# Squares of x summed by VectorE once all of x is there, and rotary tables of three mixers made behind x

## The chip, the cores and the metric

The kernel runs on one core of one Trainium2 chip. The metric is the device time of one execution in microseconds. In the rows, PE is TensorE's matmuls, PEld its weight loads, DVE is VectorE, ACT is ScalarE, POOL is GpSimd, and SP is SyncE, which here only issues the weights' DMAs. A name with a q behind it (SPq, ACTq, POOLq) is the queue of that engine.

## The reference

A sequence of 256 rows of 1024 floats (batch 1) goes through two blocks of four layers each, all in float32. In the first, every layer is a gated feed-forward part, a mixer (kinds A, B, C, A) and a second feed-forward part; in the second, a mixer (NSA, stick-breaking attention, convolution, MoBA) and an MLP.

```python
def rms_norm(x, g):
    return x * rsqrt(mean(x * x, -1) + 1e-6) * g
for i in range(4):                       # first block
    x = x + 0.5 * rms_norm(swiglu_ffn(rms_norm(x, g[0]), ...), g[1])
    x = x + rms_norm(mixer(rms_norm(x, g[2]), ...), g[3])
    x = x + 0.5 * rms_norm(swiglu_ffn(rms_norm(x, g[4]), ...), g[5])
for i in range(4):                       # second block
    x = x + mixer_2(rms_norm(x, attn_norm[i]), ...)
    x = x + square(relu(rms_norm(x, mlp_norm[i]) @ w_up)) @ w_down
```

Each of the 20 steps needs the sum of squares of x over the 1024 features of each row, and the three sub-parts of the first block also that of their own result. Mixer B turns queries and keys by tables of cosine and sine that come from an input of positions; NSA and MoBA normalise every head by its own root mean square, with a gain, and turn it by tables that the kernel has as constants.

## The kernel before

x stays in SBUF, transposed: `self.x` is [128, 8, 256], eight parts of 128 features by 256 rows. A float32 product is made of two halves of each side in three matmuls (`mm3`): `xThi` is x times the gain, rounded by ScalarE, and `xTlo` the rest, by VectorE; each weight tile comes by a DMA on SP's queue into `raw` (three buffers), ScalarE rounds it into `whi` and VectorE makes `wlo` (four buffers each). `wlo` of 128x512 is what VectorE mostly does.

A step ends in `handoff`. Where its result is normalised (a *gated* step, the twelve of the first block), `normed` gets the factor of each row, and then, part by part, VectorE multiplies the result by it (`yg<-yg,ps`) and adds it to x (`x<-x,yg`), ScalarE makes `xThi` and VectorE `xTlo`. The first four parts come one by one (128x256), the last four in two pairs (128x512). In the second block `add_y` does that in pairs, without a factor. The first matmuls of the next step (`arriving`) use the parts in the order in which they come, so TensorE can wait for each `xThi` and `xTlo`.

For the next step's row factor, `rest_x` squares each pair of parts on ScalarE (into `acc` for the first pair, into `sq` then) and `add_squares` adds it to `acc` on GpSimd: three additions of 128x512 per step. `rms` folds `acc` on GpSimd (128x256), then TensorE sums over the partitions (`col_sums`, `ps<-ones,acc`), VectorE makes `e` (mean plus a small number) and GpSimd `r = e ** -0.5`. In a feed-forward step TensorE soon turns `r` into a row over the partitions (`to_rows`, `ps<-identr,r`); in a mixer `r` scales what leaves PSUM, and in NSA and MoBA `hrx`, `rs_e`, `rs_r` and `hrs` are the factors of single heads, `rope_a` and `rope_b` the two products of a rotation, added on GpSimd and then transposed by TensorE.

In mixer B, `rope_positions` makes the tables on VectorE from `pos_i`; in NSA and MoBA `gained_rope` multiplies the constants by the gains (`qtc`, `qts` for queries; `ktc`, `kt0c` and so on for keys). Both stand in the code ahead of the first projections. Temporaries lie in `temp()`, which is the buffer `yg` (there is one).

The order on each engine is not written out. Tasks (`spawn`) are generators; `tick` after each `mm3` advances those whose time has come by a planner (`Clock`, a table of modelled costs per engine), `after` waits for other tasks, and a scheduler behind it orders each engine's queue by those modelled times. So an instruction that changes its engine also changes where others stand. Nearly every operation is recorded by one helper, so its line is L163 throughout.

Of the kernel before, what the change touches and what calls it, by code (L numbers as in the profile page):

```python
# [17 lines left out]
P = 128  # L18
D = 1024
S = 256  # L20
# [180 lines left out]
class Net:  # L201
# [337 lines left out]

    def new_stats(self):  # L540
        self.acc = self.nrm.tile([P, 2, S], F32, name="acc", bufs=1)
        self.e = self.small.tile([P, 2], F32, name="e", bufs=3)
        r = self.small.tile([P, 2], F32, name="r", bufs=3)
        self.r2, self.r = r, [r[:, t:t + 1] for t in range(2)]
# [8 lines left out]
    def rest_x(self, ks, g):  # L553

        nc = self.nc
        hi, lo = self.xTs
        for k in ks:
            ins = nc.vector.scalar_tensor_tensor(lo[:, k], self.x[:, k], self.gcol[:, k, g:g + 1], hi[:, k].bitcast(F32),
                                                 op0=ALU.mult, op1=ALU.subtract)
            if k % 2:  # L560
                self.add_squares(self.acc, self.x[:, k - 1:k + 1], k == 1)
        self.have[1] = ks[-1] + 1
        return ins

    def leave(self, b):

        x = self.x[:, 2 * b:2 * b + 2]
        for t in range(2):
# [5 lines left out]
            self.nc.sync.dma_start(self.a["out"][0, t * P:(t + 1) * P, b * S:(b + 1) * S], z)  # L574

    def arriving(self):

        for k in range(KB + LATE):
            for part, i in ((0, k), (1, k - LATE)):
                if 0 <= i < KB:  # L580
                    self.until(lambda: self.have[part] > i)
                    yield from [(i, 0, 1)] if part else [(i, 0, 0), (i, 1, 0)]

    def add_squares(self, acc, x, first, engine=None):
        nc = self.nc
        sq = acc if first else self.nrm.tile([P, 2, S], F32, name="sq", bufs=2)
        nc.scalar.activation(sq, x, AF.Square)
        if not first:
            (engine or nc.gpsimd).tensor_tensor(acc, acc, sq, op=ALU.add)

# [26 lines left out]
    def rms(self, deps):  # L617

        nc = self.nc
        yield from self.after(deps)  # L620
        nc.gpsimd.tensor_tensor(self.acc[:, 0], self.acc[:, 0], self.acc[:, 1], op=ALU.add)
        yield
        pc = self.bank()[:, :2]
        self.col_sums(pc, [self.acc[:, 0]], True, True)
        nc.vector.tensor_scalar(self.e, pc, 1.0 / D, EPS, op0=ALU.mult, op1=ALU.add)
        nc.gpsimd.tensor_tensor(self.r2, self.e, self.mhalf[:, :2], op=ALU.pow)
# [51 lines left out]
    def gain_y(self, y, ds, g, o):  # L678

        nc = self.nc  # L680
        b = ds[0] // 2
        acc = o["acc"]
        if len(ds) == 2:
            self.add_squares(acc, y[1][b], b == 0, nc.vector)
            if b == 2:
                nc.vector.tensor_tensor(acc[:, 0], acc[:, 0], acc[:, 1], op=ALU.add)
        else:
            sq = self.nrm.tile([P, 2, S], F32, name="sq", bufs=2)[:, 0]
            nc.scalar.activation(sq, y[0][ds[0]], AF.Square)
            if ds[0] == 6:  # L690
                o["add"] = nc.vector.tensor_tensor(acc[:, 0], acc[:, 0], sq, op=ALU.add)
            else:
                o["last"] = sq
        for d in {(4, 5): (), (6,): (4, 5, 6), (7,): ()}.get(ds, ds):
            ins = nc.vector.tensor_scalar(self.yg[:, d], y[0][d], self.gcol[:, d, g:g + 1], None, op0=ALU.mult)
            if d >= 4:
                self.behind(ins, o["add"])
        return
        yield

    def normed(self, y, o, g_out, g_next, weight, rest):
# [16 lines left out]
        rows = self.to_rows(r, WARM, last)  # L718
        self.new_stats()
        before = None  # L720
# [356 lines left out]
    def rope_positions(self, c):  # L1077
# [3 lines left out]
        nc.scalar.dma_start(pi, self.a["positions"].rearrange("o (t p) -> p (o t)", p=P))  # L1081
        pf = c.tile([P, 2], F32, name="pos_f")
        nc.vector.tensor_copy(pf, pi)
        tmp = self.temp()
        ang, kq, r, w = [tmp[:, i * 64:(i + 1) * 64].rearrange("p (t d) -> p t d", t=2) for i in range(4)]
# [192 lines left out]
    def mixer_b(self, mp, m1, j, kv, end):  # L1278
        nc = self.nc
        self.rope_positions(m1)  # L1280
        tabs = [m1.tile([P, 2, 64], F32, name=f"tab{t}") for t in range(2)]
# [45 lines left out]
        for jp in range(2):  # L1327
# [3 lines left out]
            for z, dst in enumerate((qT, kT)):  # L1331
                memory(jp * 3 + z)
                for t, ps in self.chunk(384):
                    if jp == 0 and z == 0:
                        for i, tab in enumerate((self.cos1, self.sin1)):
                            nc.vector.tensor_scalar(tabs[t][:, i], tab[:, t], self.r[t], None, op0=ALU.mult)
# [118 lines left out]

    def gained_rope(self, pool, gain, name):

        nc = self.nc
        c, s = [pool.tile([P, 2, P], F32, name=name + z) for z in "cs"]
        tab = lambda z: self.k[z].rearrange("p (t d) -> p t d", t=2)  # L1460
        half = lambda i: gain[:, i * 64:(i + 1) * 64].unsqueeze(1).to_broadcast([P, 2, 64])
        for i in range(2):
            nc.vector.tensor_tensor(c[:, :, i * 64:(i + 1) * 64], tab("cos2"), half(i), op=ALU.mult)
        nc.vector.scalar_tensor_tensor(s[:, :, :64], tab("sin2"), -1.0, half(1), op0=ALU.mult, op1=ALU.mult)
        nc.vector.tensor_tensor(s[:, :, 64:], tab("sin2"), half(0), op=ALU.mult)
        return c, s

# [20 lines left out]
    def nsa(self, mp, m1, stack, end):  # L1488
# [3 lines left out]
        cp = cctx.enter_context(self.tc.tile_pool(name="cmp", bufs=1))  # L1492
        tmp = self.temp()
        kg, qg = tmp[:, :3 * P], tmp[:, 3 * P:4 * P]
        nc.gpsimd.dma_start(qg, a["nsa_q_norm_2"][0].partition_broadcast(P))
        nc.gpsimd.dma_start(kg, a["nsa_k_norm_2"][0].rearrange("i d -> (i d)").partition_broadcast(P))
        qtab = self.gained_rope(m1, qg, "qt")
        ktab = [self.gained_rope(cp, kg[:, i * P:(i + 1) * P], f"kt{i}") for i in range(3)]
        kcT = cp.tile([P, 2, S], F32, name="kcT")
# [18 lines left out]

        def key(t, ps, tab, out):
            r = self.head_rms(ps, 2, t)  # L1520
            k = self.rope(mp, ps, 2, P, tab[0][:, t], tab[1][:, t])
# [228 lines left out]
    def moba(self, mp, m1, stack, end):  # L1750
        nc, a = self.nc, self.a
        sc = P ** -0.5
        gq, gk = [self.bcast_row(m1, a[f"moba_{n}_norm_2"][0], n + "g") for n in "qk"]
        qtab, ktab = self.gained_rope(m1, gq, "qt"), self.gained_rope(m1, gk, "kt")
        self.new_parts(m1, 8)

        def key(t, ps, out):
            r = self.head_rms(ps, 4, t)
            k = self.rope(mp, ps, 4, P, ktab[0][:, t], ktab[1][:, t])
# [56 lines left out]
    def prepare_conv(self, pool):  # L1816
# [6 lines left out]

        def weights():
            tmp = self.temp()[:C]
            nc.scalar.dma_start(tmp[:W], a["conv_dw_w_2"][0])
            for i, name in enumerate(("dw_b", "ln_g", "ln_b")):
                nc.scalar.dma_start(tmp[W + i:W + i + 1], a[f"conv_{name}_2"])
            yield from self.after([self.stats])
            self.clock.wait(self.clock.now() + 4 * DMA)  # L1830
# [222 lines left out]
```

## Time and profile before

| | |
|---|---|
| median of 3 runs | 3267.43 us (3265.96 to 3268.48) |
| profiled execution, its own time | 3249.1 us |
| its span, from first to last instruction | 3247.3 us |
| mean clock granted to TensorE | 0.992 |
| busy: TensorE, VectorE, ScalarE, GpSimd | 3176.4, 2109.8, 1663.0, 230.1 us |

The profiled execution is a single one, and its own time stands beside the span of the profile; durations are read from it, while times of kernels are compared by medians of runs. An engine with a small share can still hold up others at one place, so the share is read first and the order of time afterwards.

### The profile page before, as it was taken

What the parts mean: (1) busy time and instruction counts of PE and PEld (TensorE: products, weight loads), DVE (VectorE), ACT (ScalarE), POOL (GpSimd) and SP (SyncE); (2) the same over time, 40 slices, a digit from 0 to 9 for tenths busy, and PEclk for the clock granted to TensorE, in tenths of its full rate; (3) what the DMA queues carried; (4) which work ended last, traced back from release to release, by engine and by line L of the source; (5) the groups of instructions that cost most, each with busy time, mean ns of one, the idle gap of its engine ahead of it and who ended that gap; (6) DMA issues with size and microseconds to landing.
All of it is one profiled execution on the core that took longest, in us unless ns stands there. A gap on an engine that the chain in (4) does not pass through costs nothing. (4 is left out here: it accounts for less than half of the span.)

```text
span 3247.3 us, 60685 instructions
## 1 busy us (share of the span) xinstructions
PE 3176.4 (98%) x25234; PEld 3028.7 (93%) x25234; DVE 2109.8 (65%) x3877; ACT 1663.0 (51%) x3396; POOL 230.1 (7%) x205
## 2 busy tenths in 40 slices
PE   8999999999999999999999999999999999999999
PEld 8998999998999997899998998799989999997998
DVE  5657757566757556665757756775667576657754
ACT  6445545444545445544545544645565464545643
POOL 1001000001000000000001001200102010002100
PEclk9999999999999999999999999999999999999999
DMA  7654555544454643365554654536545551554463
GB/s 265 209 195 156 169 195 171 193 130 149 155 193 155 212 157 124 117 208 182 183 195 137 196 195 136 182 104 195 177 162 175 189 182 40 189 188 154 140 201 130
DMA packets 387971, 550.89 MB, mean 170 GB/s; under 512 B 12109, under 2 KB 310957, under 8 KB 387695
## 3 DMA queue, kind: packets, MB, share of 16 engines
q1 hardware_dynamic: 372648, 534.89, 50.4%
q10 hardware_dynamic: 14694, 10.92, 1.1%
q8 instruction: 198, 3.24, 0.4%
q0 software_dynamic: 352, 1.19, 0.2%
q14 instruction: 79, 0.64, 0.1%
HBM read 543.82 MB, written 3.15 MB: 168 GB/s over the span
## 5 line engine op out<-in xcount | busy, mean ns | idle before, releaser
L163 ACT CAST whi<-raw 128x512 fp32r<-128x512 f32 x1996 | 1119.1, 617 | 1041.5 <-issue 870.4
L163 DVE TENSOR_TENSOR wlo<-raw,whi 128x512 fp32r<-128x512 f32 x1996 | 1307.6, 700 | 509.7 <-ACT whi L163 508.7
L163 PE MATMUL ps<-xThi,whi 128*128 128x256 f32 x3904 | 1037.7, 278 | 3.3 <-ACT xThi L163 3.3
L163 PE MATMUL ps<-xTlo,whi 128*128 128x256 f32 x3904 | 1033.9, 277 | 4.5 <-DVE xTlo L163 4.5
L163 PE MATMUL ps<-xThi,wlo 128*128 128x256 f32 x3904 | 1032.8, 277 | 0.0
L163 PEld LDWEIGHTS ps<-xTlo,whi 128*128 128x128 f32 x3904 | 713.3, 188 | 6.4 <-DVE xTlo L163 5.9
L163 PEld LDWEIGHTS ps<-xThi,whi 128*128 128x128 f32 x3904 | 713.0, 188 | 6.7 <-ACT xThi L163 6.1
L163 PEld LDWEIGHTS ps<-xThi,wlo 128*128 128x128 f32 x3904 | 713.5, 188 | 0.0
L163 PE MATMUL ps<-hTlo,whi 128*128 128x256 f32 x2176 | 602.8, 277 | 0.0
L163 PE MATMUL ps<-hThi,wlo 128*128 128x256 f32 x2176 | 602.7, 277 | 0.0
L163 PE MATMUL ps<-hThi,whi 128*128 128x256 f32 x2176 | 602.7, 277 | 0.0
L163 PEld LDWEIGHTS ps<-hThi,wlo 128*128 128x128 f32 x2176 | 409.6, 188 | 0.0
L163 PEld LDWEIGHTS ps<-hThi,whi 128*128 128x128 f32 x2176 | 409.4, 188 | 0.0
L163 PEld LDWEIGHTS ps<-hTlo,whi 128*128 128x128 f32 x2176 | 409.4, 188 | 0.0
L163 PE MATMUL ps<-whi,xThi 128*128 128x512 f32 (+4 forms) x688 | 255.1, 386 | 4.6 <-ACT xThi L163 4.6
L163 PE MATMUL ps<-whi,xTlo 128*128 128x512 f32 (+4 forms) x688 | 245.4, 372 | 4.7 <-DVE xTlo L163 4.7
L163 PE MATMUL ps<-wlo,xThi 128*128 128x512 f32 (+4 forms) x688 | 245.0, 372 | 2.0 <-DVE wlo L163 1.9
L163 DVE TENSOR_TENSOR act<-ps,rows 128x512 f32<-128x512 f32 x88 | 60.7, 690 | 179.2 <-PE ps L163 179.2
L163 DVE TENSOR_TENSOR h<-ps,act 128x512 f32<-128x512 f32 x88 | 60.8, 690 | 149.3 <-PE ps L163 145.7
L163 PEld LDWEIGHTS ps<-whi,xTlo 128*128 128x128 f32 x688 | 130.5, 191 | 26.5 <-DVE xTlo L163 7.3
L163 PEld LDWEIGHTS ps<-whi,xThi 128*128 128x128 f32 x688 | 130.1, 192 | 26.0 <-ACT xThi L163 8.2
L163 POOL TENSOR_TENSOR acc<-acc,sq 128x512 f32<-128x512 f32 x60 | 95.1, 1586 | 828.2 <-issue 637.3
(332 smaller groups left out, 3495.5 us busy)
## 6 DMA issues: line engine op xcount, KB each, us to landing
raw<-in_ffn_w_gate_up_dram SPq DMA_DIRECT2D x176, 1024.0 KB, 5.1
raw<-in_ffn_w_down_dram SPq DMA_DIRECT2D x88, 1024.0 KB, 4.9
raw<-in_mlp_w_up_dram SPq DMA_DIRECT2D x64, 1024.0 KB, 5.5
raw<-in_mlp_w_down_dram SPq DMA_DIRECT2D x64, 1024.0 KB, 4.9
raw<-in_a_w_in_dram SPq DMA_DIRECT2D x12, 1024.0 KB, 5.2
raw<-in_sb_w_in_dram SPq DMA_DIRECT2D x12, 1024.0 KB, 5.1
raw<-in_moba_w_in_dram SPq DMA_DIRECT2D x12, 1024.0 KB, 5.1
raw<-in_b_w_in_dram SPq DMA_DIRECT2D x36, 256.0 KB, 3.7
```

Of the source, the lines that this page charges most:

```text
L163: return f(*args, **kw)
```

## The change

GpSimd no longer adds squares. ScalarE writes the squares of all four pairs into `yg`; when all of x is there, VectorE adds the eight parts in place in three additions (128x1024, 128x512, 128x256), and TensorE sums what is left. In the gated steps `yg` is the buffer out of which the same parts of x were just made. The tables of mixer B, NSA and MoBA become tasks of their own that begin when all of x has been split (`arrived`), in tiles `sq` instead of `yg`; NSA's gains come by ScalarE's DMA queue instead of GpSimd's, and MoBA's keys and NSA's keys wait for the tables (`tabled`). The convolution's small weights are fetched behind the statistics. The diff, cut to its core (the calls of the gates' own `add_squares`, which ran on VectorE already, only lose an argument):

```diff
-    def new_stats(self):
-        self.acc = self.nrm.tile([P, 2, S], F32, name="acc", bufs=1)
+    def new_stats(self, squares=None):
+
+        self.squares = self.nrm.tile([P, KB, S], F32, name="yg", bufs=1) if squares is None else squares
...
             if k % 2:
-                self.add_squares(self.acc, self.x[:, k - 1:k + 1], k == 1)
+                nc.scalar.activation(self.squares[:, k - 1:k + 1], self.x[:, k - 1:k + 1], AF.Square)
...
+    def arrived(self):
+
+        while self.have[1] < KB:
+            yield 0
+        self.clock.wait(self.clock.now())
+        yield
...
-            (engine or nc.gpsimd).tensor_tensor(acc, acc, sq, op=ALU.add)
+            nc.vector.tensor_tensor(acc, acc, sq, op=ALU.add)
...
         yield from self.after(deps)
-        nc.gpsimd.tensor_tensor(self.acc[:, 0], self.acc[:, 0], self.acc[:, 1], op=ALU.add)
+        s = self.squares
+        for n in (4, 2, 1):
+            nc.vector.tensor_tensor(s[:, :n], s[:, :n], s[:, n:2 * n], op=ALU.add)
         yield
         pc = self.bank()[:, :2]
-        self.col_sums(pc, [self.acc[:, 0]], True, True)
+        self.col_sums(pc, [s[:, 0]], True, True)
...
-        self.new_stats()
+        self.new_stats(self.yg)
...
+        tmp = self.nrm.tile([P, 2, S], F32, name="sq", bufs=2).rearrange("p j n -> p (j n)")
+        yield from self.arrived()
         nc.vector.tensor_copy(pf, pi)
-        tmp = self.temp()
...
-        self.rope_positions(m1)
+        tables = self.spawn(self.rope_positions(m1))
...
+                        self.finish([tables])
...
-        nc.gpsimd.dma_start(qg, a["nsa_q_norm_2"][0].partition_broadcast(P))
-        nc.gpsimd.dma_start(kg, a["nsa_k_norm_2"][0].rearrange("i d -> (i d)").partition_broadcast(P))
-        qtab = self.gained_rope(m1, qg, "qt")
-        ktab = [self.gained_rope(cp, kg[:, i * P:(i + 1) * P], f"kt{i}") for i in range(3)]
+        nc.scalar.dma_start(qg, a["nsa_q_norm_2"][0].partition_broadcast(P))
+        nc.scalar.dma_start(kg, a["nsa_k_norm_2"][0].rearrange("i d -> (i d)").partition_broadcast(P))
...
+        def tables():
+            yield from self.arrived()
+            for tab, g in zip(ktab + [qtab], [kg[:, i * P:(i + 1) * P] for i in range(3)] + [qg]):
+                self.gained_rope(tab, g)
+
+        tabled = self.spawn(tables())
...
         def key(t, ps, tab, out):
+            yield from self.after([tabled])
...
-        qtab, ktab = self.gained_rope(m1, gq, "qt"), self.gained_rope(m1, gk, "kt")
+        qtab, ktab = [self.rope_tiles(m1, name) for name in ("qt", "kt")]
...
+        def tables():
+            yield from self.arrived()
+            self.gained_rope(ktab, gk)
+            self.gained_rope(qtab, gq)
+
+        tabled = self.spawn(tables())
...
         def weights():
+            yield from self.after([self.stats])
             tmp = self.temp()[:C]
...
-            yield from self.after([self.stats])
```

What stands on VectorE at the entrance of a feed-forward step (the third of the program's twenty entrances; the six others behind gated steps read the same), from the last `xTlo` to `e`, before:

```order
L163 TENSOR_TENSOR wlo<-raw,whi 128x512
L163 SCALAR_TENSOR_TENSOR xTlo<-x,gcol,xThi 128x256 x2
L163 TENSOR_TENSOR wlo<-raw,whi 128x512 x6
L163 TENSOR_SCALAR e<-ps 128x2
L163 TENSOR_TENSOR wlo<-raw,whi 128x512
L163 TENSOR_SCALAR rest<-e 128x2
```

and in the changed kernel:

```order
L163 TENSOR_TENSOR wlo<-raw,whi 128x512
L163 SCALAR_TENSOR_TENSOR xTlo<-x,gcol,xThi 128x256 x2
L163 TENSOR_TENSOR yg<-yg 128x1024
L163 TENSOR_TENSOR wlo<-raw,whi 128x512
L163 TENSOR_TENSOR yg<-yg 128x512
L163 TENSOR_TENSOR wlo<-raw,whi 128x512
L163 TENSOR_TENSOR yg<-yg 128x256
L163 TENSOR_TENSOR wlo<-raw,whi 128x512
L163 TENSOR_SCALAR e<-ps 128x2
L163 TENSOR_TENSOR wlo<-raw,whi 128x512
L163 TENSOR_SCALAR rest<-e 128x2
```

The three additions stand among the `wlo` between the last `xTlo` and `e`. Of the six `wlo` that stood there two remain ahead of the last addition and one between it and `e`; three are behind `e` now.

On VectorE at the entrance of mixer B, the stretch of the last parts of x, before (`yg<-cf,pos_f` and `yg<-yg` of 128x64 make the tables):

```order
L163 TENSOR_TENSOR x<-x,yg 128x512
L163 SCALAR_TENSOR_TENSOR xTlo<-x,gcol,xThi 128x256
L163 TENSOR_SCALAR yg<-cf,pos_f 128x32 x2
L163 TENSOR_TENSOR wlo<-raw,whi 128x512
L163 TENSOR_SCALAR yg<-yg 128x64
L163 SCALAR_TENSOR_TENSOR xTlo<-x,gcol,xThi 128x256
L163 TENSOR_SCALAR yg<-yg 128x64
L163 SCALAR_TENSOR_TENSOR xTlo<-x,gcol,xThi 128x256
L163 TENSOR_SCALAR yg<-yg 128x64
L163 TENSOR_TENSOR wlo<-raw,whi 128x512
```

and in the changed kernel (the tables' temporaries are now `sq`; five of their operations stand ahead of the first part of x and three among its early parts, above this piece):

```order
L163 TENSOR_TENSOR x<-x,yg 128x512
L163 SCALAR_TENSOR_TENSOR xTlo<-x,gcol,xThi 128x256
L163 SCALAR_TENSOR_TENSOR sq<-sq 128x64
L163 TENSOR_TENSOR wlo<-raw,whi 128x512
L163 SCALAR_TENSOR_TENSOR xTlo<-x,gcol,xThi 128x256 x2
L163 TENSOR_SCALAR sq<-sq 128x64
L163 TENSOR_TENSOR yg<-yg 128x1024
L163 TENSOR_SCALAR sin_8439<-sin_8439 128x2x32
L163 TENSOR_SCALAR sq<-sq 128x64
L163 TENSOR_TENSOR wlo<-raw,whi 128x512
L163 COPY cos_8438<-cos_8438 128x2x32
```

Of the table operations only one is left between the last `x` and the last `xTlo`, where four stood.

On VectorE behind the entrance of MoBA, around `e`, before (`ktc`, `kts` are tables of keys, `qtc`, `qts` of queries):

```order
L163 TENSOR_TENSOR ktc<-cf,kg 128x2x64 x2
L163 SCALAR_TENSOR_TENSOR kts<-cf,kg 128x2x64
L163 TENSOR_TENSOR kts<-cf,kg 128x2x64
L163 TENSOR_TENSOR wlo<-raw,whi 128x512 x13
L163 TENSOR_SCALAR e<-ps 128x2
L163 TENSOR_SCALAR hrx<-r 128x1 x12
L163 TENSOR_SCALAR rs_e<-hms 128x4
L163 TENSOR_TENSOR rope_a<-ps,ktc 128x512
L163 TENSOR_SCALAR hrs<-rs_r,hrx 128x4
L163 TENSOR_TENSOR rope_b<-ps,kts 128x4x64 x2
```

and in the changed kernel:

```order
L163 TENSOR_TENSOR yg<-yg 128x256
L163 TENSOR_TENSOR wlo<-raw,whi 128x512 x8
L163 TENSOR_SCALAR e<-ps 128x2
L163 TENSOR_TENSOR wlo<-raw,whi 128x512
L163 TENSOR_SCALAR hrx<-r 128x1 x8
L163 TENSOR_TENSOR wlo<-raw,whi 128x512
L163 TENSOR_SCALAR hrx<-r 128x1
L163 TENSOR_TENSOR wlo<-raw,whi 128x512
L163 TENSOR_SCALAR hrx<-r 128x1 x3
L163 TENSOR_TENSOR wlo<-raw,whi 128x512 x2
L163 TENSOR_SCALAR rs_e<-hms 128x4
L163 TENSOR_TENSOR rope_a<-ps,qtc 128x512
```

Thirteen `wlo` stood ahead of `e`; now fifteen and the three additions do (five `wlo` and the two larger additions stand above this piece). The first group of heads that is turned behind `e` is one of queries instead of keys. On TensorE the second and third of the four first groups of turned heads stood three matmuls apart; now 33 lie between them, and six between the third and the fourth where there were also six.

## Rows read from the trace of the kernel before

**Rows 1.** The page, busy time (us, share, instructions) of each engine.
```profile
PE 3176.4 (98%) x25234; PEld 3028.7 (93%) x25234; DVE 2109.8 (65%) x3877; ACT 1663.0 (51%) x3396; POOL 230.1 (7%) x205
```

**Rows 2.** PE's waits, whole span (last row: 2736 to 2746): us, times, longest.
```profile
PE ps L163 <- DVE xTlo L163: 9.2, 12, 1.8
...
PE ps L163 <- ACT xThi L163: 8.0, 13, 1.7
PE ps L163 <- POOL rope_a L163: 7.9, 3, 7.4
...
PE ps L163 <- POOL r L163: 5.1, 7, 0.8
...
PE ps L163 <- ACT xThi L163: 1.3, 1, 1.3
```

**Rows 3.** Order of time, 340 to 355 us, DVE and POOL: start us, us.
```profile
340.52 0.48 DVE L163 SCALAR_TENSOR_TENSOR xTlo<-x,gcol,xThi 128x256 fp32r<-128x256 f32 x1
...
341.91 1.78 DVE L163 TENSOR_TENSOR x<-x,yg 128x512 f32<-128x512 f32 x1
...
345.69 1.76 DVE L163 TENSOR_TENSOR wlo<-raw,whi 128x512 fp32r<-128x512 f32 x1
347.38 2.39 DVE L163 SCALAR_TENSOR_TENSOR xTlo<-x,gcol,xThi 128x256 fp32r<-128x256 f32 x2
349.68 3.69 DVE L163 TENSOR_TENSOR wlo<-raw,whi 128x512 fp32r<-128x512 f32 x6
353.30 0.15 DVE L163 TENSOR_SCALAR e<-ps 128x2 f32<-128x2 f32 x1
...
341.80 1.34 POOL L163 TENSOR_TENSOR acc<-acc,sq 128x512 f32<-128x512 f32 x1 [5.92 <-issue]
...
353.52 1.11 POOL L163 TENSOR_TENSOR r<-e,mhalf 128x2 f32<-128x2 f32 x1 [4.04 <-DVE e L163]
```

**Rows 4.** Order of time, same stretch, PE; in brackets idle before, and releaser.
```profile
344.28 0.74 PE L163 MATMUL ps<-xThi,whi 128*128 128x256 f32 x4 [0.20 <-ACT xThi L163]
...
348.94 0.74 PE L163 MATMUL ps<-xTlo,whi 128*128 128x256 f32 x4 [0.63 <-DVE xTlo L163]
...
350.88 0.50 PE L163 MATMUL ps<-ones,acc 128*128 128x1 f32 x4
...
354.68 0.49 PE L163 MATMUL ps<-identr,r 128*128 128x128 f32 x2 [0.72 <-POOL r L163]
```

**Rows 5.** POOL's groups by form: busy us in all, mean ns of one.
```profile
L163 POOL TENSOR_TENSOR acc<-acc,sq 128x512 f32<-128x512 f32 x60 | 95.1, 1586 | 828.2 <-issue 637.3 <-ACT sq L163 190.6
...
L163 POOL TENSOR_TENSOR acc<-acc 128x256 f32<-128x256 f32 x20 | 17.6, 879 | 1.6
```

**Rows 6.** VectorE's groups by form, the additions in steps with a gate.
```profile
L163 DVE TENSOR_TENSOR acc<-acc,sq 128x512 f32<-128x512 f32 x24 | 16.6, 692 | 15.7 <-ACT sq L163 15.7
...
L163 DVE TENSOR_TENSOR acc<-acc,sq 128x256 f32<-128x256 f32 x12 | 5.1, 425 | 1.2
```

**Rows 7.** Order of time at mixer B's entrance, DVE and PE.
```profile
722.17 1.41 DVE L163 TENSOR_SCALAR yg<-cf,pos_f 128x32 f32<-128x32 f32 x2
...
725.80 0.61 PE L163 MATMUL ps<-whi,xTlo 128*128 128x384 f32 x2 [1.77 <-DVE xTlo L163]
```

**Rows 8.** NSA's entrance: order of time; DMA issues, KB each, median us to landing.
```profile
2003.03 0.38 ACT L163 ACTIVATE sq<-ps 128x256 f32<-128x256 f32 x1 [0.98 <-PE ps L163]
...
2005.84 0.42 DVE L163 TENSOR_TENSOR yg<-yg,ps 128x256 f32<-128x256 f32 x1 [1.18 <-PE ps L163]
...
yg<-in_nsa_q_norm_dram POOLq DMA_DIRECT2D x1, 64.0 KB, 3.1
```

**Rows 9.** Windows (PE, PEld, DVE, ACT, POOL, PEclk, DMA, GB/s) and PE in moba.
```profile
726.00:732.00 6.00, 6.00 (x27) 6.00 (x27) 6.00 (x18) 2.31 (x7) 0.34 (x1) 0.72 0.38 109
2984.00:2990.00 6.00, 5.95 (x24) 5.13 (x25) 3.69 (x5) 1.69 (x3) 1.67 (x1) 0.54 0.47 155
...
2984.05 1.11 PE L163 MATMUL ps<-identr,rope_a 128*128 128x128 f32 x4 [7.43 <-POOL rope_a L163]
```

More of the change, by code (lines that the diff above doesn't have):

```diff
@@ L582, in arriving, with add_squares @@
                     yield from [(i, 0, 1)] if part else [(i, 0, 0), (i, 1, 0)]
-    def add_squares(self, acc, x, first, engine=None):
+    def add_squares(self, acc, x, first):
         nc = self.nc
@@ L1454, in mixer2, with rope_tiles, gained_rope @@
             (self.nsa, self.stick, self.conv, self.moba)[i](mp, m1, stack, (None, g_next))
-    def gained_rope(self, pool, gain, name):
+    def rope_tiles(self, pool, name):
+        return [pool.tile([P, 2, P], F32, name=name + z) for z in "cs"]
+    def gained_rope(self, tab, gain):
         nc = self.nc
-        c, s = [pool.tile([P, 2, P], F32, name=name + z) for z in "cs"]
-        tab = lambda z: self.k[z].rearrange("p (t d) -> p t d", t=2)
+        c, s = tab
+        const = lambda z: self.k[z].rearrange("p (t d) -> p t d", t=2)
         half = lambda i: gain[:, i * 64:(i + 1) * 64].unsqueeze(1).to_broadcast([P, 2, 64])
         for i in range(2):
[L1463 to L1466, printed above, removed]
+            nc.vector.tensor_tensor(c[:, :, i * 64:(i + 1) * 64], const("cos2"), half(i), op=ALU.mult)
+        nc.vector.scalar_tensor_tensor(s[:, :, :64], const("sin2"), -1.0, half(1), op0=ALU.mult, op1=ALU.mult)
+        nc.vector.tensor_tensor(s[:, :, 64:], const("sin2"), half(0), op=ALU.mult)
     def head_rms(self, src, n, t, scale=1.0):
@@ L1492, in nsa @@
         cp = cctx.enter_context(self.tc.tile_pool(name="cmp", bufs=1))
-        tmp = self.temp()
+        tmp = self.nrm.tile([P, 2, S], F32, name="sq", bufs=2).rearrange("p j n -> p (j n)")
         kg, qg = tmp[:, :3 * P], tmp[:, 3 * P:4 * P]
-        nc.gpsimd.dma_start(qg, a["nsa_q_norm_2"][0].partition_broadcast(P))
-        nc.gpsimd.dma_start(kg, a["nsa_k_norm_2"][0].rearrange("i d -> (i d)").partition_broadcast(P))
-        qtab = self.gained_rope(m1, qg, "qt")
-        ktab = [self.gained_rope(cp, kg[:, i * P:(i + 1) * P], f"kt{i}") for i in range(3)]
+        nc.scalar.dma_start(qg, a["nsa_q_norm_2"][0].partition_broadcast(P))
+        nc.scalar.dma_start(kg, a["nsa_k_norm_2"][0].rearrange("i d -> (i d)").partition_broadcast(P))
+        tabs = [self.rope_tiles(pool, name) for pool, name in ((m1, "qt"), (cp, "kt0"), (cp, "kt1"), (cp, "kt2"))]
+        qtab, ktab = tabs[0], tabs[1:]
+        def tables():
[3 more added lines that the diff above has]
+        tabled = self.spawn(tables())
         kcT = cp.tile([P, 2, S], F32, name="kcT")
@@ L1753, in moba @@
         gq, gk = [self.bcast_row(m1, a[f"moba_{n}_norm_2"][0], n + "g") for n in "qk"]
-        qtab, ktab = self.gained_rope(m1, gq, "qt"), self.gained_rope(m1, gk, "kt")
+        qtab, ktab = [self.rope_tiles(m1, name) for name in ("qt", "kt")]
[4 more added lines that the diff above has]
+        tabled = self.spawn(tables())
         self.new_parts(m1, 8)
         def key(t, ps, out):
+            yield from self.after([tabled])
             r = self.head_rms(ps, 4, t)
```

2 lines of the change are left out of this document (1 added, 1 removed).

## The prediction

> **What bounds the kernel now.** The page's first section comes first: TensorE is busy 98% of the span, VectorE 65%, ScalarE 51%, GpSimd 7% [rows 1]. As a total VectorE can take more work, and GpSimd's own busy time is not what ends the run. What can be gained stands in TensorE's idle time of 71 us (3247.3 - 3176.4), so the second view is for whom TensorE waited [rows 2]. Three entries touch the change: xTlo of VectorE, 9.2 us in 12 waits, xThi of ScalarE, 8.0 us in 13, and `r` of GpSimd, 5.1 us in 7. All but one of the xThi waits (1.3 us at the end of the convolution mixer) lie where a step hands x to the next one. The fourth is rope_a of GpSimd, of which one wait is 7.4 us. The rest (startup, exponents, compressed keys) lies outside the change.
>
> The third view is the order of time at one such entrance, 340 to 355 us, one of seven like it where a gated step ends and a feed-forward step begins. GpSimd begins its first addition of squares at 341.80; VectorE's `x` of 128x512, begun 0.11 us later, takes 1.78 us [rows 3], while an addition of that shape takes 0.69 on VectorE as a mean over 24 elsewhere [rows 6]. A `wlo` at 345.69 takes 1.76, beside GpSimd's second addition, where six in a row later take 3.69 together; the last two xTlo take 2.39, where one at 340.52 takes 0.48. TensorE pays 0.20 us at 344.28 for xThi and 0.63 at 348.94 for xTlo [rows 4]. Then the sums of squares run on TensorE at 350.88, but VectorE has the six `wlo` ahead of `e`, which begins at 353.30; GpSimd's `r` takes 1.11, and TensorE stands 0.72 us at 354.68. So the limit is no engine's busy share, but two late places in VectorE's queue.
>
> **The change part by part. GpSimd's additions go.** 60 of mean 1586 ns and 20 of mean 879 ns, 112.7 us of GpSimd [rows 5]. Nothing of TensorE's list above waits for them by name; what they cost is VectorE's stretching, 1.1 us for that `x` alone. Most of it is covered, and what is not is the wait at the entrances, 9.2 + 8.0 - 1.3 = 15.9 us. In the entrance above, 1.1 us comes off the first `x`, 1.1 off the `wlo`, and 2.39 becomes about 0.9 (two at 0.48, partly overlapped); the last xTlo then ends near 346.1 instead of 349.8 (347.38 + 2.39), and neither gap is left. Mixer B is the widest case, 1.77 us for xTlo alone [rows 7], because the table operations stand in VectorE's queue before the last two xTlo (1.41 us for the first pair). With them on either side of that stretch some 0.4 us stays. In the NSA mixer the changed order itself puts table operations (128x128, so under the 0.43 us of 128x256) between the early parts of x, so I let 1.5 us stay. Gain: 15.9 - 0.4 - 1.5 = **14.0 us**; bounds 15.9 if all goes, and about 5 if the additions on GpSimd explain only half of the xTlo part.
>
> **Three additions per step for VectorE.** 128x256 takes 425 ns and 128x512 692 ns in rows of the same operation [rows 6]; 267 ns more for 256 columns, so 128x1024 is put at 692 + 2 x 267 = 1226 ns, an estimate worked out from these. One set is 2.35 us, 20 sets 47 us of VectorE; bounds 42 (starts that overlap by 0.08 us, as six `wlo` in 3.69 us do against 0.69 each) and 58 (if the largest is stretched to 1.76). VectorE goes to at most 67% of the span. The cover: at the feed-forward entrances they take the place of three of the six `wlo` ahead of `e`, as the order shows; three `wlo` and three additions behind the last xTlo, 346.1 + 3 x 0.62 + 2.2, put `e` near 350.2. The sums of squares wait for the last addition, near 349.5; TensorE arrives near 349.85 (350.88 less 0.83 of gaps and 0.2 of slow first matmuls). That margin is only 0.3 us. If the cover is gone, each entrance pays what is missing: 1 us late is 7 us in all.
>
> **`r` at the seven feed-forward entrances.** With `e` near 350.2 and 1.11 us for `r`, it is there at 351.4. TensorE has 27 matmuls instead of 21 between the sums and the transposes of `r`. The sums and the 21 took 3.08 us (350.88 to 354.68 less the 0.72), so with 27 it asks near 349.85 + 3.8 = 353.6, 2 us later than needed. All **5.1 us** go; bounds 0 and 5.1.
>
> **Tables and queries of moba.** TensorE stands 7.43 us at 2984.05 for the third group of rotated heads, which it reaches three matmuls after the second; over the 6 us behind it the granted clock is 0.54 [rows 9]. In the changed order the queries come first, 33 projection matmuls lie between the second and the third group, and six before the fourth. Replayed with the durations of before (`e` some 2 us later, then the same chain of statistics, rotation and GpSimd addition) the first two groups are ready about 2 and 1 us ahead of need, the last two about level. I take 6 of the 7.4 us; bounds 0 (the stall comes back at another group) and 7.4. **Clock:** behind this stall 6 x 0.46 = 2.8 us were lost, behind mixer B's gaps 6 x 0.28 = 1.7 us; I count **4 us**, bounds 0 and 4.5. Together **10 us**.
>
> **What becomes later.** In the eight mixers the sums of squares come some 24 to 41 matmuls later in TensorE's order, about 4 to 7 us, and `e` stands behind 11 to 16 `wlo` and the additions instead of 7 to 13. Behind `e` on VectorE wait the per-head factors; behind them `r`, rotated and normalised heads, then TensorE. The cover is the projections, which need only x. In the stick and convolution mixers it looks ample; in A, B, C and NSA it ends close to the first transposes. At the very first entrance the transposes of `r` have 19 matmuls ahead instead of 52. Bounds: nothing, and, by the nearest row, at one mixer a stall like moba's with its clock, 7.4 + 2.8 = 10.2 us. I take **4 us** lost in all, nearer the lower end, since of three waits for rotated heads before only one was long (7.4 of 7.9 us). In it are NSA's gains, which now leave from ScalarE's queue: the tile `sq` is free and ScalarE idle after its last square at 2003.03 + 0.38, so the first is issued near 2003.4 [rows 8]. If it lands 3.1 us later, as from GpSimd's queue, it is there at 2006.5; VectorE would want it at 2005.84 + 0.42, so waits 0.3 us, and for the second transfer up to 1 us. The Trainium skill's page "DMA: Bandwidth & Descriptors", section "Anatomy of one DMA — SWDGE (gpsimd) path", gives for a transfer issued by GpSimd about 2.0 us fixed plus the bytes over 436 GB/s: for these 64 KB an estimate of 2.15 us, no wait here and a sum 0.3 us better. The trace's 3.1 us for the same transfer does not agree, and the sum goes by the trace. ScalarE's squares stay in number and shape, only their destination differs: zero.
>
> **Sum.** 14.0 + 5.1 + 10.0 - 4.0 = 25 us. The profiled execution took 3249.1 us, 18.3 under the median of 3267.4; so 3224 us against the one is **3242 us** against the other.
>
> **The rivals.** (1) *The entrances gain, the heads do not*: 14 + 5, but moba's stall and slow clock come back at another group and the 4 us of later statistics are paid: 15 us, 3252. For it: moba's `e` still stands behind `wlo` whose weights must land first. Against: 33 matmuls of new cover. (2) *The change only moves the work*: the sums wait for a chain of additions behind the last xTlo instead of one that ran on GpSimd meanwhile. If that chain ends 1.8 us later than replayed, the seven entrances pay 7 x (1.8 - 0.3), 10 of their 19 us, back; with moba unchanged and 4 us of later statistics 5 us remain, 3262, and with 9 us of them nothing, 3267. For it: the margin of 0.3 us. Against: VectorE's 0.69 us against GpSimd's 1.59 for the same addition. (3) *Slower: late statistics in the mixers.* `e` behind 14 to 16 `wlo`, which wait for weights, starves TensorE at rotated heads or exponents at 10.2 us each, moba's price. Against the 29 us of gains it decides from the third mixer on; at four, with moba's own gain gone, 19 stand against 41: 3289. For it: moba did just that. Against: the other mixers showed no such wait.
>
> **How the numbers follow.** Forecast 0.60, its own range 3229 (15.9 + 5.1 + 7.4 + 4.5 us, no new wait, and 5 us of other waits that happen to go) to 3249; rival 1 0.20, rival 2 0.12, rival 3 0.08. Range 3229 to 3264, which leaves out rival 3 and part of rival 2. A measurement of this kernel can tell 0.2%, 6.5 us, from no change. Faster: forecast, rival 1 and a quarter of rival 2, 0.83; within 0.2%: 0.09; slower: rival 3, 0.08.
>
> **What would show it.** Right: GpSimd near 120 us busy; `x` of 128x512 near 0.69 us each; TensorE's waits for xTlo and xThi under 4 us together; none for `r` at the feed-forward entrances; none for rope_a over 2 us; a granted clock of 1.00 behind moba's transposes. Wrong: a new TensorE wait for `yg` at the sums of squares at each entrance (rival 2), or for `r`, rope_a or exponents of several us in mixers that had none (rival 3).

## The result, and the profile after

The changed kernel took 3226.48 us as the median of 4 runs (3223.20 to 3239.98), the kernel before 3266.69 beside it (3262.36 to 3268.48): ratio 0.9895, 95% interval 0.9870 to 0.9919, so 1.05% or 34 us faster. Measured twice more on other chips it gave 0.9943 (0.9923 to 0.9963) and 0.9912 (0.9886 to 0.9938). The intervals of the first and the second do not meet: single executions of one program differ here by 20 to 30 us, in part for a reason that comes to light below. The mean of the three ratios is 0.9917, 27 us, beside the 25 us of the forecast.

The page of the profiled execution (span 3238.1 us), busy times of the engines as in [rows 1]:

```profile
PE 3183.6 (98%) x25234; PEld 3044.8 (94%) x25234; DVE 2093.7 (65%) x3937; ACT 1661.3 (51%) x3396; POOL 117.9 (4%) x123
```

GpSimd lost 112.2 us, as worked out. VectorE took on 60 additions and still is busy 16 us less. TensorE's idle time, span less busy, is 54.5 us instead of 70.9; but it is busy 7.2 us longer with the same 25234 matmuls, which no step of the prediction has.

For whom TensorE waited, the same view as [rows 2]:

```profile
PE ps L163 <- ACT p L163: 16.8, 6, 5.1
...
PE ps L163 <- DVE rope_a L163: 3.6, 5, 1.1
PE ps L163 <- ACT xThi L163: 2.6, 4, 1.3
...
PE ps L163 <- POOL rope_a L163: 1.9, 3, 1.0
...
PE ps L163 <- DVE yg L163: 0.6, 3, 0.2
```

xTlo and `r` are gone from the list, xThi has 2.6 us of which the convolution's 1.3 never was at stake. rope_a of GpSimd fell from 7.9 to 1.9. In their place stand the waits for exponents (`p` of ScalarE), 16.8 us, and rope_a's products on VectorE, 3.6 us. The exponents' line of before:

```profile
PE ps L163 <- ACT p L163: 8.8, 7, 2.6
```

VectorE's groups by form, which answer to [rows 6], and those that were stretched before:

```profile
L163 DVE SCALAR_TENSOR_TENSOR xTlo<-x,gcol,xThi 128x256 fp32r<-128x256 f32 x160 | 73.1, 480 | 3.6 <-ACT xThi L163 3.6
L163 DVE TENSOR_TENSOR yg<-yg 128x1024 f32<-128x1024 f32 x20 | 24.4, 1219 | 0.0
L163 DVE TENSOR_TENSOR x<-x,yg 128x512 f32<-128x512 f32 x24 | 16.4, 685 | 0.0
L163 DVE TENSOR_TENSOR yg<-yg 128x512 f32<-128x512 f32 x20 | 13.7, 685 | 0.0
L163 DVE TENSOR_TENSOR yg<-yg 128x256 f32<-128x256 f32 x20 | 8.4, 418 | 0.0
```

and these last, `xTlo` and `x`, before:

```profile
L163 DVE SCALAR_TENSOR_TENSOR xTlo<-x,gcol,xThi 128x256 fp32r<-128x256 f32 x160 | 101.1, 653 | 3.6 <-ACT xThi L163 3.6
L163 DVE TENSOR_TENSOR x<-x,yg 128x512 f32<-128x512 f32 x24 | 29.6, 1232 | 0.0
```

The addition of 128x1024 takes 1219 ns where 1226 was estimated, the three together 46.5 us. The entrance that [rows 3] and [rows 4] show, in order of time, VectorE first, then TensorE and GpSimd:

```profile
340.07 0.69 DVE L163 TENSOR_TENSOR x<-x,yg 128x512 f32<-128x512 f32 x1
...
343.37 0.88 DVE L163 SCALAR_TENSOR_TENSOR xTlo<-x,gcol,xThi 128x256 fp32r<-128x256 f32 x2
344.16 1.22 DVE L163 TENSOR_TENSOR yg<-yg 128x1024 f32<-128x1024 f32 x1
...
347.11 0.42 DVE L163 TENSOR_TENSOR yg<-yg 128x256 f32<-128x256 f32 x1
...
348.33 0.50 PE L163 MATMUL ps<-ones,yg 128*128 128x1 f32 x4
348.87 0.16 DVE L163 TENSOR_SCALAR e<-ps 128x2 f32<-128x2 f32 x1 [0.74 <-PE ps L163]
...
349.11 1.09 POOL L163 TENSOR_TENSOR r<-e,mhalf 128x2 f32<-128x2 f32 x1 [15.70 <-DVE e L163]
...
351.96 0.61 PE L163 MATMUL ps<-identr,r 128*128 128x128 f32 x4
```

`x` takes 0.69 instead of 1.78, the last two xTlo 0.88 instead of 2.39. The last addition ends at 347.53, 0.8 us before TensorE wants it; `e` waits for TensorE instead of for `wlo`; `r` is there at 350.20, 1.8 us ahead of its transposes. At three of the seven entrances (four in the two later profiles) TensorE does stand for the last addition, 0.2 us each (`yg` above): the margin of 0.3 us was as thin as it was put.

MoBA's waits of TensorE, which answer to the last line of [rows 9]:

```profile
2983.26 0.63 PE L163 MATMUL ps<-identr,rope_a 128*128 128x128 f32 x4 [1.07 <-DVE rope_a L163]
2993.19 1.35 PE L163 MATMUL ps<-identr,p 128*128 128x128 f32 x3 [5.10 <-ACT p L163]
```

The 7.43 us for rotated heads became 1.07; ten us later TensorE stands 5.10 us for the first exponents.

### The profile page after: what moved, and what is told of

Same layout as the page of the kernel before. It is cut to its first block, busy times and chain, and to the rows that moved or that the text cites. A ratio compares the mean times of both kernels' runs of the same rounds, so it can differ in the third digit from the quotient of the medians.

```text
span 3238.1 us, 60602 instructions
## 1 busy us (share of the span) xinstructions
PE 3183.6 (98%) x25234; PEld 3044.8 (94%) x25234; DVE 2093.7 (65%) x3937; ACT 1661.3 (51%) x3396; POOL 117.9 (4%) x123
## 5 line engine op out<-in xcount | busy, mean ns | idle before, releaser
L163 PEld LDWEIGHTS ps<-wlo,xThi 128*128 128x128 f32 x688 | 130.3, 190 | 16.8
```

Source lines behind the costliest of these rows:

```text
L163: return f(*args, **kw)
```

## The experiments

The theory behind the prediction: VectorE was held up by GpSimd's additions while it made the parts of x. Rivals: it is the moment of the sums that counts, or the place of the tables, whatever engine adds. The kernels ran on three chips: the two unaltered ones, the sums alone and the tables alone on the first; the sums on GpSimd, the sums pair by pair, no additions and the wait for `r` on the second; the rest on the third. Each ratio is against runs of the kernel before on the same chip. TensorE's idle time, span less busy from each page, is given beside the ratio: it is 70.9 and 74.1 us in two profiles of the kernel before and 54.5, 55.1 and 54.6 in three of the changed one, so a difference of idle time well over 3 us tells programs apart where single times do not.

**The two kernels again.** Both unaltered.

> The changed kernel once more, unaltered, to see what differs between two executions of one program. In its first profile three feed-forward steps (842 to 1023, 1361 to 1531, 1822 to 2003 us) ran their 128x256 matmuls one every 117.8 ns, the other ones every 113.5 ns; in the kernel before all seven such steps behind gated steps ran at 113.5. If that pitch is drawn anew in each execution, another set of steps is slow now and the median lies at 3222 to 3230 us, 36 to 45 us under the kernel before. If it is fixed by the order of the instructions, the same three steps are slow again and the profiled execution is again near 3240.

> The kernel before once more, unaltered: ratio 1.000 with 0.3% to each side. Its first profiled execution was 18 us under its median. If the pitch of the matmuls is drawn anew, this profile has some feed-forward steps at 117.8 ns and a time nearer to 3267; if it is fixed, none, and a time near 3249.

The changed kernel: 3236.06 us, ratio 0.9943 (0.9923 to 0.9963), some 19 us faster where 36 to 45 were expected; the kernel before against itself 0.9991 (0.9978 to 1.0004). The profiled execution of the changed kernel took 3249.94 us, that of the kernel before 3248.49: nothing gained in this pair, though idle time is 55.1 us against 74.1. The rest is in the matmuls themselves. Windows inside four feed-forward steps, changed kernel, second profile (columns as in [rows 9], with the number of instructions in parentheses):

```profile
400.00:500.00 100.00, 100.00 (x851) 100.00 (x851) 56.28 (x90) 45.44 (x84) 0.00 (x0) 1.00 0.56 189
880.00:1000.00 120.00, 120.00 (x1021) 120.00 (x1020) 65.66 (x105) 53.22 (x98) 0.00 (x0) 1.00 0.56 186
1400.00:1500.00 100.00, 100.00 (x851) 100.00 (x851) 55.82 (x90) 44.47 (x83) 0.00 (x0) 1.00 0.57 186
1860.00:1960.00 100.00, 100.00 (x852) 100.00 (x851) 54.83 (x88) 44.05 (x82) 0.00 (x0) 1.00 0.56 184
```

The first two of these windows in the first profile of the kernel before:

```profile
400.00:500.00 100.00, 100.00 (x885) 100.00 (x884) 56.59 (x91) 45.74 (x85) 0.00 (x0) 1.00 0.58 191
880.00:1000.00 120.00, 120.00 (x1062) 120.00 (x1061) 69.37 (x111) 55.93 (x103) 0.00 (x0) 1.00 0.58 194
```

and in the third profile of the changed kernel, which comes further below:

```profile
400.00:500.00 100.00, 100.00 (x885) 100.00 (x884) 56.82 (x91) 45.63 (x84) 0.00 (x0) 1.00 0.58 191
880.00:1000.00 120.00, 120.00 (x1061) 120.00 (x1061) 69.45 (x112) 56.10 (x104) 0.00 (x0) 1.00 0.58 193
```

TensorE is busy without a break at a granted clock of 1.00 (2.4 GHz) in all three, and starts 851 matmuls of 128x256 in 100 us in the first and 885 in the others: one every 117.5 or every 113.0 ns. A step of this kind holds some 170 us of them, so one that runs slow costs 170 x (1 - 113.0/117.5) = 6.5 us. In the first profile of the changed kernel three steps ran slow, in the second four, in the third none. So in the changed kernel this pace (the expectations say pitch) is drawn anew in each execution, and the set of slow steps isn't fixed by the program. The two profiles of the kernel before had no slow step; its expectation had named that as the sign of a fixed pace, and that it is drawn there too is not shown.

**The sums alone.** The tables are made at once, between the parts of x:

```diff
     def arrived(self):
 
-        while self.have[1] < KB:
-            yield 0
-        self.clock.wait(self.clock.now())
+        return
         yield
...
+        self.finish([tables])
...
+        self.finish([tabled])
```

> The changed kernel with the tables of mixer B, NSA and MoBA made at once between the parts of x, as before; the squares stay with VectorE behind x. Theory (GpSimd's additions held VectorE up): TensorE's waits for xTlo and xThi fall from 17.2 to 5 or 6 us, none for r is left, MoBA's 7.4 us stall and mixer B's table wait stay: about 17 to 20 us under the kernel before, 3247 to 3250. Rival (the tables' place is what counts): at most 5 us under it.

3240.89 us, ratio 0.9957 (0.9938 to 0.9976), idle 56.6 us: by the ratio some 14 us, less than the 17 to 20 expected, beside the changed kernel's 0.9943 on this chip; by idle time nearly all of the change's gain, without the tables' move. Waits for xThi 4.8 us (3.1 of it at NSA, where VectorE now makes tables for 3.2 us between the first `yg` and the first `x`), none for xTlo, none for `r`. Two expectations failed: mixer B's wait for xTlo did not stay, and MoBA's stall of 7.4 us did not either, so the tables' place had not caused it. With the later sums alone TensorE's order in MoBA is the changed kernel's to the last instruction, and the 5.1 us for exponents come instead, as there.

**The tables alone.** GpSimd adds squares as in the kernel before:

```diff
+        self.acc = self.nrm.tile([P, 2, S], F32, name="acc", bufs=1)
...
-                nc.scalar.activation(self.squares[:, k - 1:k + 1], self.x[:, k - 1:k + 1], AF.Square)
+                self.add_squares(self.acc, self.x[:, k - 1:k + 1], k == 1, nc.gpsimd)
...
+        nc.gpsimd.tensor_tensor(self.acc[:, 0], self.acc[:, 0], self.acc[:, 1], op=ALU.add)
```

> The kernel before with only the tables moved behind x; the squares are added by GpSimd as before (the tables have a buffer of their own in mixer B, NSA's gains still come by GpSimd's queue once x is there). Theory: the seven feed-forward entrances still wait for xTlo, xThi and r, about 11 us in all, mixer B's 1.8 us wait for xTlo goes and MoBA's stall as well: 6 to 11 us under the kernel before, 3256 to 3261. Rival (the tables' place is what counts): 25 us or more under it.

3263.19 us, ratio 1.0029 (1.0015 to 1.0044), idle 76.7 us: slower, where 6 to 11 us of gain were expected. The entrances are as before (xTlo 9.7 us, xThi 8.6, `r` 5.4); of mixer B's 1.77 us for xTlo 1.55 stay. Changed are, among the waits (before: none; 7.9 us, of which 7.4 in MoBA; 2.8 us):

```profile
PE ps L163 <- DVE rope_a L163: 6.5, 3, 4.3
...
PE ps L163 <- POOL rope_a L163: 5.1, 2, 4.2
PE ps L163 <- DMA wcmp<-in_nsa_w_cmp_dram: 4.4, 1, 4.4
```

Of the waits for rotated heads the longest, 4.3 us, is in MoBA, and it is none for tables: these are done at 2970.71, and the first head uses them at 2982.90. The next, 4.2 us, is in NSA, where the tables, done at 2029.68, stand behind `e`. TensorE's order is another one in both mixers; why these waits came is not shown. The rival that the tables' place is what counts is out.

**The same sums behind x, on GpSimd.**

```diff
         for n in (4, 2, 1):
-            nc.vector.tensor_tensor(s[:, :n], s[:, :n], s[:, n:2 * n], op=ALU.add)
+            nc.gpsimd.tensor_tensor(s[:, :n], s[:, :n], s[:, n:2 * n], op=ALU.add)
```

> The changed kernel with its three additions given to GpSimd: squares still wait for all of x, but GpSimd adds them. Theory (what cost time was GpSimd adding while VectorE made x): the waits for xTlo and xThi are gone as in the changed kernel, under 4 us; the additions take about 2.9, 1.5 and 0.9 us, some 3 us longer than on VectorE, and show as TensorE's waits at the sums or for r of 1 to 3 us at the seven feed-forward entrances, 10 to 20 us in all, so about as long as the kernel before. Rival (the engine matters, not the moment): xTlo and xThi waits stay near 16 us.

3260.88 us, ratio 1.0040 (1.0025 to 1.0054), idle 73.6 us. xTlo takes 479 ns and `x` of 128x512 683, xThi's waits are 2.9 us and xTlo's gone: with GpSimd idle while x is made, VectorE is undisturbed. But TensorE waits 17.8 us for `yg` of GpSimd at the sums. Keeping GpSimd out of that stretch frees x; doing the sums on VectorE is what keeps them from being late.

**The sums pair by pair, on VectorE.** As in the tables-only kernel, with the additions (and the fold of `acc`) on VectorE:

```diff
-                self.add_squares(self.acc, self.x[:, k - 1:k + 1], k == 1, nc.gpsimd)
+                self.add_squares(self.acc, self.x[:, k - 1:k + 1], k == 1)
...
-        nc.gpsimd.tensor_tensor(self.acc[:, 0], self.acc[:, 0], self.acc[:, 1], op=ALU.add)
+        nc.vector.tensor_tensor(self.acc[:, 0], self.acc[:, 0], self.acc[:, 1], op=ALU.add)
```

> The sums as in the kernel before, pair by pair while x arrives, but on VectorE instead of GpSimd; tables behind x as in the tables-only kernel. Theory: xTlo back at 0.48 us and x of 128x512 at 0.69, but 0.69 us additions now stand among them; TensorE's waits for xTlo and xThi between 5 and 12 us, none for r at the feed-forward entrances; 8 to 15 us under the kernel before. Rival (only having the sums behind x counts): as the tables-only kernel, about 10 us over the kernel before.

3227.59 us, ratio 0.9929 (0.9908 to 0.9949), idle 57.0 us: the same gain with the sums not behind x at all. The waits are 2.7 us for xThi and 0.3 for xTlo, less than the 5 to 12 expected, and the gain of some 23 us is above the expected 8 to 15. At the entrance of 333 to 350 us two of the additions, 0.68 us each, stand among the parts (339.80 and 342.39) in a VectorE without idle time, and TensorE, with matmuls of earlier parts ahead of it, does not stand there at all. The rival that only the moment counts is out.

**No additions.**

```diff
         s = self.squares
-        for n in (4, 2, 1):
-            nc.vector.tensor_tensor(s[:, :n], s[:, :n], s[:, n:2 * n], op=ALU.add)
```

> The changed kernel without the three additions: the sums go over the first of eight parts alone, so the row factors are not those of the reference. What the additions cost in all. Theory (they are covered at the feed-forward entrances and cost up to 5 us by later statistics in the mixers): 0 to 8 us under the changed kernel at the same chip, the waits for exponents (ACT p, 16.8 us in the changed kernel) near the 8.8 us of before. Rival (47 us more of VectorE are felt everywhere): 15 us or more under it.

3206.34 us, ratio 0.9867 (0.9846 to 0.9889), idle 44.8 us, waits for exponents 7.0. Against the 54.7 us of the changed kernel the 46.5 us of additions cost 10 us of TensorE's idle time, nearly all of it in the mixers, where `e` now comes late (the waits for exponents are 9.8 us of it); at the feed-forward entrances they are covered. By the ratios (0.9867 on one chip, against the mean of 0.9917 on three) the time fell by 16 us, above the 0 to 8 expected and at the edge of the rival's 15; no step was slow in this profile and TensorE's order is another one too, so part of it may be the draw of the pace or the order.

**Useless additions put back.** ScalarE halves the squares of three pairs, GpSimd doubles them; TensorE's order is the changed kernel's to the last instruction:

```diff
+                z, extra = self.squares[:, k - 1:k + 1], k < KB - 1
-                nc.scalar.activation(self.squares[:, k - 1:k + 1], self.x[:, k - 1:k + 1], AF.Square)
+                nc.scalar.activation(z, self.x[:, k - 1:k + 1], AF.Square, scale=0.5 ** 0.5 if extra else 1.0)
+                if extra:
+                    nc.gpsimd.engine.tensor_tensor(z, z, z, op=ALU.add)
```

> The changed kernel with three additions of 128x512 per step put back on GpSimd while x arrives, for no use: ScalarE scales the first three pairs' squares by a half, GpSimd doubles them in place (z + z), 60 additions like those of before; VectorE's sums and TensorE's order are those of the changed kernel. Theory (GpSimd's additions hold VectorE up): x of 128x512 and xTlo stretch again, to about 1000 and 550 ns or more, and TensorE's waits for xTlo, xThi and for yg at the sums grow by 6 to 14 us over the 3.3 us of the changed kernel. Rival (what gained was the later sums or the tables): they stay within 2 us of it.

> The changed kernel unaltered, on the chip of the three others, as their measure: 0.991 to 0.996 of the kernel before, three or four feed-forward steps at 117.8 ns in the profile.

The changed kernel: 3226.76 us, ratio 0.9912 (0.9886 to 0.9938), idle 54.6 us, no slow step where three or four were expected. With the useless additions: 3260.72 us, ratio 1.0020 (1.0003 to 1.0037), idle 72.9 us. The whole gain is gone. Its entrance in order of time, VectorE, GpSimd and TensorE:

```profile
338.66 1.14 POOL L565 TENSOR_TENSOR yg<-yg 128x512 f32<-128x512 f32 x1 [1.43 <-ACT yg L163]
338.83 1.53 DVE L163 TENSOR_TENSOR x<-x,yg 128x512 f32<-128x512 f32 x1
...
340.95 0.74 PE L163 MATMUL ps<-xThi,whi 128*128 128x256 f32 x4 [0.54 <-ACT xThi L163]
...
341.90 1.04 POOL L565 TENSOR_TENSOR yg<-yg 128x512 f32<-128x512 f32 x1 [2.09 <-ACT yg L163]
341.93 1.29 DVE L163 SCALAR_TENSOR_TENSOR xTlo<-x,gcol,xThi 128x256 fp32r<-128x256 f32 x1
...
344.54 1.22 DVE L163 TENSOR_TENSOR yg<-yg 128x1024 f32<-128x1024 f32 x1
...
348.04 0.58 PE L163 MATMUL ps<-ones,yg 128*128 128x1 f32 x4 [1.17 <-DVE yg L163]
```

and its waits:

```profile
PE ps L163 <- ACT xThi L163: 9.6, 14, 1.5
PE ps L163 <- DVE yg L163: 9.5, 8, 1.3
...
PE ps L163 <- DVE xTlo L163: 1.3, 4, 0.5
```

`x` and xTlo beside an addition end 0.56 and 0.28 us after it; their means are 1104 and 600 ns. The three waits are 20.4 us together, 16.9 more than the 3.5 in the third profile of the changed kernel, above the 6 to 14 expected. The wait for `yg` at the sums is not one for GpSimd's results: its last addition ends at 342.94, and VectorE begins the first sum 1.6 us later, when it is through with xTlo. So the contention is shown directly.

**What sets the pace.** In the steps looked at it holds from the transposes of `r` to the end of the step, and at these transposes TensorE no longer waits. First a wait was put back there; then the transposes were set 6 and 9 matmuls later.

```diff
+        hold = 4 if getattr(self, "following", None) is not None and self.following[0] == "ffn" else 0
...
+        for _ in range(hold):
+            nc.gpsimd.engine.tensor_tensor(self.r2, self.r2, self.ones[:, :2], op=ALU.mult)
```

> The changed kernel with r multiplied by ones four times on GpSimd (about 0.65 us each) at the seven feed-forward entrances behind gated steps, unknown to the planner, so that TensorE's order stays as it is and TensorE stands idle about 0.7 to 1 us before the transposes of r. Theory of the pitch (a step's matmuls come every 113.5 or every 117.8 ns, decided at the transposes of r, and an idle TensorE there makes 113.5 likely): in the profile none or one of the seven steps at 117.8, against three and four in the two profiles of the changed kernel; waits for r 5 to 7 us; the profiled execution 12 to 18 us under that of the changed kernel at the same chip. Rival (the pitch has nothing to do with the wait): three or four steps stay at 117.8 and the time rises by the 5 to 7 us of waits.

3232.51 us, ratio 0.9946 (0.9928 to 0.9965), idle 59.1 us. TensorE waits 5.4 us for `r` in 7 places, and three steps still run slow: idleness does not bring the fast pace, and that theory falls.

```diff
                     cols = self.r2
+                    self.clock.wait(self.clock.chain + 0.64)
```

> The changed kernel with the transposes of r six matmuls later on TensorE at the seven feed-forward entrances (33 instead of 27 behind the sums; a constant of 0.64 us added to the planner's time of that task). No work is added or removed. Theory (which of the two pitches a feed-forward step runs at hangs on where in TensorE's order the transposes stand): with 33, as in the kernel that adds squares on VectorE as x comes, none or one of the seven steps at 117.8 ns in the profile, where the changed kernel had three and four; its profiled execution 12 to 24 us under that of the changed kernel on this chip, TensorE's idle time the same within 2 us. Rival (chance, or something else in the changed kernel): three or four steps stay slow, profiled execution the same within 6 us.

> The same with the transposes nine matmuls later (36 behind the sums). If any place but 27 gives the fast pitch, as 33 above; if the place decides as such, it may be either, and the seven steps agree among themselves more than chance would have it.

Six later: 3236.26 us, ratio 0.9937 (0.9913 to 0.9961), one slow step. Nine later (0.9 us): 3228.20 us, ratio 0.9919 (0.9893 to 0.9945), none. But the unaltered kernel had none on that chip either, so these tell nothing of the place; idle time is 53.8 and 54.0 us. No version is shown to beat the changed kernel.

## Why the prediction was right, point by point

**The limit.** Right: two late places in VectorE's queue, not a share. The durations came back to the undisturbed ones (480 and 685 ns, where the rows had 0.48 us and 692 ns), and the useless additions took the gain away again. The Trainium skill's page "SBUF — State Buffer", section "SBUF: two separate sides", says that a VectorE instruction with two inputs in SBUF and a GpSimd instruction that reads SBUF exclude one another for the whole of the one that began first. The trace agrees: the `x` that began 0.11 us behind GpSimd's addition ended at 343.69, 0.55 us after that addition [rows 3], so of its 0.69 us at most 0.14 were done in the 1.23 us beside it.

**GpSimd's additions go, 14.0 us.** Right: 17.2 us of waits for x became 2.6, so 14.6. What was put in for NSA (1.5 us) was 0.9, for B 0.4 as said. The reason given for mixer B was wrong: in the tables-only kernel no table operation stands between VectorE's x parts there, and TensorE still waits 1.55 us for xTlo and 1.50 for xThi; so most of it was GpSimd's additions there too.

**Three additions, covered.** Right in size (46.5 for 47 us) and place; VectorE's busy time even fell, since 60 additions cost less than the stretching that went.

**`r`, 5.1 us.** Right, all of it.

**MoBA and the clock, 10 us.** The stall for rotated heads went as foretold (7.9 to 1.9 us over the whole kernel), with the new order of the heads that was given as the reason; but that order comes with the later sums and not with the tables, as the kernel of the sums alone shows. And it came back at the next thing that hangs on `e`: 5.10 us for exponents and 1.28 for the heads' results. In MoBA 7.45 us stand against 8.84 (7.43, 0.98 and 0.43), a gain of 1.4 where 6 were counted. The clock fell again behind the new wait: it was 0.50 (1.2 GHz) over 2991.98 to 2998.81 us, 3.4 us lost, and before 0.50 over 2979.26 to 2989.50, 5.1 us, so 1.7 came back. Behind mixer B's entrance it still was 0.58 over 742 to 746 us in the first profile, and 1.00 in the other two. Over the whole span, where 0.001 of the mean granted clock is 3.2 us, nothing of the 4 us is to be seen on the average: it was 0.992 in both profiles of the kernel before and 0.992, 0.991 and 0.993 in the three of the changed one. This is rival 1's mechanism, and it was true of this part.

**What becomes later, 4 us lost.** Mis-sized: waits for exponents rose by 8.0 us, 4.7 of it in MoBA (there a sign that the prediction named for being wrong), those for rope_a on VectorE by 3.6, six smaller ones together by about 4; some 15.7 us in all. On the other side, about 6 us of waits outside the sum also went (compressed keys' weights 2.6, `wlo` 1.9, others 1.7). The bound for one mixer, 10.2 us, was sound; that A, NSA and MoBA each pay a few was not seen. The gains of NSA by ScalarE's queue made no wait: issued at 1996.8 to 1997.5, they were in use at 1999.96 and 2000.83 without idle time ahead, so landing took at most 3.2 and 3.4 us, and the 0.3 to 1 us that was put in for it was not paid.

**The sum.** 16.4 us of TensorE's idle time were gained (70.9 to 54.5) where the parts had 21 of it and 4 of clock; that is nearer to rival 1's 15 us than to the forecast. The three ratios stand for 34, 19 and 29 us. What lies beyond 16 us is in the matmuls: in the three profiled executions of the changed kernel TensorE was busy 3183.6, 3193.0 and 3161.7 us, a spread of 31 us with an idle time that agrees within 0.6; three and four slow steps at 6.5 us make 20 and 26 of it.

The third of these and the two profiles of the kernel before, all without a slow step, can be compared. Their spans are 3216.3 against 3247.3 and 3246.7 us, and of the 30 us between them 11 to 15 are busy time. Some 7 of these lie in the seven feed-forward steps behind gated ones. Seven windows, each from one gate's sums of squares to the next gate's, in the first profile of before and in the third of the changed kernel:

```profile
sum 1318.70, PE 1306.75 PEld 1296.97 DVE 843.17 ACT 645.82 POOL 49.30; mean PE 186.68 PEld 185.28 DVE 120.45 ACT 92.26 POOL 7.04
...
sum 1300.50, PE 1299.15 PEld 1292.74 DVE 832.36 ACT 644.84 POOL 12.40; mean PE 185.59 PEld 184.68 DVE 118.91 ACT 92.12 POOL 1.77
```

The seven steps became 18 us shorter, 10.6 of it idle and 7.6 busy time, which the prediction put at nothing. About half of that is clock: at the steps behind mixers B and C it was 0.50 for 3.4 us (835.69 to 839.10 and 1351.10 to 1354.51 us), in the second profile of the kernel before too, and in no profile of the changed one. And the four matmuls behind a wait for x take 0.74 us [rows 4] where the next four take 0.63. What the rest is stays open.

So the forecast's 25 us, beside 27 by the mean of the ratios, was met by 16 us of idle time, less than summed since two terms were mis-sized, and by some 10 us of busy time that it did not have in it: that the number agrees so well is luck. In the profiles it was the changed kernel that had the slow steps, and the pace of executions without a profile can't be seen.

## What to carry to other kernels

GpSimd, busy 7%, held up VectorE, busy 65%, where both read SBUF at the same moment: look at single durations beside the other engine's instructions, not at shares, and put such work on the busier engine if it has a gap there. A statistic that is made later is paid for at the first thing that hangs on it, and when a stall is taken away there, the next consumer has it; so follow the chain to the exponents before the gain is counted. And where single executions scatter by a per cent, compare the idle time of the limiting engine between profiles: here it agreed within 0.6 us in three profiles of one program and 3.2 us in two of another, while times differed by 20 to 30 us.

## What was not expected of the hardware

TensorE runs the same stream of 128x256 matmuls at two paces, one every 112.8 to 113.6 or one every 117.3 to 117.5 ns (count of a window into its length), at a granted clock of 1.00 and without idle time, and keeps the pace for a whole step of 170 us. Of the seven steps behind gated ones, the second feed-forward step of each of the four layers can run at either pace, and in the changed kernel draws it anew in each execution: slow were 3, 4 and 0 of these four in three executions of the changed kernel, 3 with a wait of 0.7 us put ahead of them, 0 and 0 in the kernel before, and 0 or 1 in the other kernels. The other three were at about 113.5 in every profile. What decides it is not settled: an idle TensorE ahead of the step does not, and for the place of the transposes, six or nine matmuls later, nothing was shown. Nor does the wait of 0.2 us at the sums: the slow steps of the first two profiles all had it, but in the third all four steps had it and none was slow, and with the wait for `r` the first of the slow steps had none.
